# Four seven-product pairs instead of three in every second group of the first feed-forward matrix, weight sums made in place, and an earlier turn of the results

## The chip, the cores and the metric

The kernel runs on one core of one Trainium2 chip. The metric is the device time of one execution in microseconds, from its first instruction to its last. Three runs of the kernel before took 2599.51, 2600.13 and 2600.87 us; their median is 2600.13 us.

## The reference

A trunk of two decoder layers on one sequence of 256 tokens, model width 2048, in float32. Each layer runs a token mixer and then a SwiGLU feed-forward; before each of the two stands an RMS norm with a scale and a shift that are made from a conditioning vector, and the result times a gate is added to the residual. What the change touches is the feed-forward of the second layer (called layer 1):

```python
def swiglu(h, w_in, w_out):
    a, b = jnp.split(h @ w_in, 2, axis=-1)
    return (jax.nn.silu(a) * b) @ w_out
...
        h = (rms_norm(x, norm2_g[i]) * (1.0 + sc2) + sh2).astype(x.dtype)
        x = (x + g2 * swiglu(h, ffn_w_in[i], ffn_w_out[i])).astype(x.dtype)
```

Here `h` is 256 x 2048, `w_in` is 2048 x 11264 (a gate half and an up half of 5632 columns) and `w_out` is 5632 x 2048.

## The kernel before, in words

**Numbers.** Every weight and every activation is held as two rounded parts, `hi` (a cast) and `lo` (the rest), and a product is three matmuls: hi by hi, hi by lo and lo by hi (lines 1188, 1189 and 1190 here, called a triple).

**Feed-forward of layer 1.** Its columns are cut into two parts of 20 and 24 tiles of 128. In each part the first matrix is worked through in groups of four tiles (512 gate columns and 512 up columns with all 2048 rows of `w_in`), then the second matrix with what came out. Group 0 is done in another, narrower form together with the norm (function `normed`); groups 1 to 4 (first part) and 5 to 10 (second part) go through `token_products`: tokens are on the output partitions, 512 weight columns move through TensorE in one matmul. The 2048 rows are taken as eight pairs of 128 rows, 0 to 7. A **plain pair** is 2 rows x 2 column blocks x 2 token halves, each a triple: 24 matmuls of 128x512. A **seven** is the same 2x2x2 block product by Winograd's scheme with seven products in place of eight: 21 matmuls, at the price of sums of weight blocks and of sums of activation blocks. In each of the ten groups three pairs are sevens: 2, 4 and 6. The order of the pairs is 0 to 7, so sevens and plain pairs alternate: P P S P S P S P. The second matrix has twelve sevens more, in three runs of four, never next to one another. A sum over sevens is kept in PSUM banks of its own (m1, m5, m6, m7) and is folded in at the group's end by VectorE (lines 1239 to 1242), after the last seven.

**Weights.** A chunk of 1 MB (128 x 2048: a pair's four blocks of 512, b11, b12, b22, b21 by the order of `Group.blocks`) is loaded by SyncE into one of three `raw` buffers. The function `prepare` makes one piece ready: ScalarE casts `hi` (line 413) and VectorE subtracts to get `lo` (line 416). There are four buffers each of `hi` and `lo` (PART_BUFS). `take`, called by the matmuls, keeps AHEAD = 2 pieces prepared beyond the one in use. A plain pair is two pieces of 1024 columns. A seven is four pieces: p0 with 512 (b11), p1 with 1024, p2 and p3 with 1024 each (sums of blocks). The sums of blocks are made by VectorE in a tile of their own, `sums`: a subtraction of 128x1024 (line 419) after p0, one of 128x512 each at lines 423 and 425; line 425 takes what line 423 made.

**Sums of activations.** `seven_sums` (lines 630 to 642) makes four sums of 128x128 (lines 636 to 639), casts them on ScalarE and subtracts 128x512 (line 642). For the first matrix this is done once for each flagged pair, while the norm's group 0 runs (`modulated`, called by `more` in `normed`); the results are `rows4`, `rows8`, `rows12`. For the second matrix it is done for each pair of tiles that comes out (`msums`, in `turned`).

**A group's end.** What is left after a group's matmuls is queued as asides, which the next group's `token_products` calls by a count (`ticked`): one row of a plain pair, 12 matmuls, counts 8, one product of a seven counts 2. `product_of(0)` is called at a count of 8, `product_of(1)` 8 later and `turned` another 16 later, so at 32, behind the first two plain pairs. `product_of` adds the plain banks to the values (line 1249), takes the silu on ScalarE and multiplies (line 1274); `turned` transposes the result on TensorE (eight matmuls, line 1260) into two banks, from which ScalarE and VectorE make hi and lo (lines 1281, 1282) and, for some tiles, ScalarE copies the bank to `full` (line 1285) for `seven_sums`. These banks are then used for the m sums of the group that runs.

**The end of group 0.** In `normed` the matmuls write two banks, whose reading on VectorE (line 705) comes after `more` has made all rows of `h` (lines 604 and 612, one each for each tile of `h`) and their sums. TensorE's next work (a transpose at line 466 and then the next narrow product) takes such a bank.

The program is written in an order that a tile framework keeps for each engine, with a priority for some instructions. [...]

## Time and profile before

| | us |
|---|---|
| runs shown | 2599.51, 2600.13, 2600.87 |
| median | 2600.13 |
| the profiled execution, whole | 2598.36 |
| its span (first to last instruction) | 2596.6 |
| busy in the span: PE, weight loads | 2566.0, 2237.0 |
| busy in the span: VectorE (DVE), ScalarE (ACT) | 2181.2, 1299.3 |

The profiled execution is 1.77 us under the median, and 1.76 us of it lie outside its span. Its records give start and duration of each instruction; a matmul's records overlap, because the next starts before the last one's end, so that what TensorE needs for one is the distance from start to start. In brackets behind a record stands how long the engine was idle before it, and what released it. The feed-forward of layer 1 lies from about 1871 us to 2583 us of the span; one group of the first matrix takes 42.72 us there.

### The profile page before, as it was taken

The numbers are of one execution on the slowest core, as the hardware profiler recorded it, in microseconds if no ns is written. First come the engines' busy times: TensorE is split into PE (matmuls) and PEld (weight loads), VectorE is DVE, ScalarE is ACT, GpSimd is POOL, SyncE is SP. The second block draws the span as 40 slices with busy tenths as digits, with TensorE's granted clock in tenths as the row PEclk, the third lists the DMA queues.
The fourth block names the chain that finished last, engine by engine and source line by source line (L and its number), as shares of the span: only waits on it lengthen the run. The fifth ranks groups of instructions, "written<-read, shape, count | busy, mean of one in ns | idle before, by whom it ended". The sixth has DMA issues, their size and how long they took to land.

```text
span 2596.6 us, 36680 instructions
## 1 busy us (share of the span) xinstructions
PE 2566.0 (99%) x14329; PEld 2237.0 (86%) x14329; DVE 2181.2 (84%) x2754; ACT 1299.3 (50%) x1757; POOL 133.3 (5%) x230
## 2 busy tenths in 40 slices
PE   7999999999999999999999999999999999999998
PEld 5998889888889888888888898888898888888887
DVE  7998878787698887777878889988899998999984
ACT  5544543444456454334444454444565554555553
POOL 0000000110000011010000000000000000000000
PEclk9999999999999999999999999999999999999999
DMA  9976668777676887878877868877755555555553
GB/s 398 402 279 242 233 240 311 277 294 278 243 296 245 319 339 290 310 286 293 304 296 282 305 242 317 322 289 285 284 185 202 191 207 201 187 203 195 195 197 128
DMA packets 96945, 687.48 MB, mean 265 GB/s; under 512 B 10753, under 2 KB 12545, under 8 KB 13825
## 3 DMA queue, kind: packets, MB, share of 16 engines
q1 hardware_dynamic: 96194, 684.48, 71.2%
q8 instruction: 112, 1.84, 0.3%
q10 hardware_dynamic: 576, 0.66, 0.1%
q14 instruction: 63, 0.52, 0.1%
HBM read 682.99 MB, written 2.10 MB: 264 GB/s over the span
## 4 chain that ended last, share of the span: by engine, by line
PE 70%; issue 28%; DMA 1%; DVE 1%; ACT 0%; SPq 0%; POOL 0%; POOLq 0%; ACTq 0%; DVEq 0%
PE bank L475 30%; PE bank L478 15%; PE bank L513 4%; PE bank L514 4%; PE bank L515 4%; PE bank L498 2%; PE bank L500 2%; PE bank L499 2%; PE bank L543 1%; PE bank L542 1%; PE bank L541 1%; PE bank L688 1%; PE bank L689 1%; PE bank L690 1%; PE bank L1055 1%
## 5 line engine op out<-in xcount | busy, mean ns | idle before, releaser
L413 ACT CAST hi<-raw 128x1024 fp32r<-128x1024 f32 (+1 forms) x912 | 932.5, 1031 | 904.8 <-PE bank L475 312.7
L416 DVE TENSOR_TENSOR lo<-raw,hi 128x1024 fp32r<-128x1024 f32 (+1 forms) x912 | 1081.8, 1196 | 285.6 <-ACT hi L413 283.2
L475 PE MATMUL bank<-h,hi 128*128 128x512 f32 x2016 | 699.8, 391 | 0.0
L478 PE MATMUL bank<-h,lo 128*128 128x256 f32 x2016 | 564.4, 280 | 0.0
L475 PEld LDWEIGHTS bank<-h,hi 128*128 128x128 f32 x2016 | 377.0, 187 | 82.5
L327 DVE SCALAR_TENSOR_TENSOR raw<-raw,cb 128x2048 f32<-128x2048 f32 x160 | 365.8, 2286 | 20.3 <-DMA raw<-w_mod 19.9
L478 PEld LDWEIGHTS bank<-h,lo 128*128 128x128 f32 x2016 | 381.0, 189 | 0.0
L475 PE MATMUL bank<-mid,hi 128*128 128x512 f32 x922 | 320.0, 394 | 0.0
L478 PE MATMUL bank<-mid,lo 128*128 128x256 f32 x922 | 255.4, 277 | 0.0
L475 PEld LDWEIGHTS bank<-mid,hi 128*128 128x128 f32 x922 | 172.9, 188 | 40.1
L513 PE MATMUL bank<-hi,h 128*128 128x512 f32 x512 | 201.5, 394 | 0.0
L514 PE MATMUL bank<-lo,h 128*128 128x512 f32 x512 | 200.6, 392 | 0.0
L515 PE MATMUL bank<-hi,h 128*128 128x512 f32 x512 | 199.7, 390 | 0.0
L1188 PE MATMUL bank<-hi,h 128*128 128x512 f32 x490 | 191.5, 391 | 0.0
L1190 PE MATMUL bank<-hi,h 128*128 128x512 f32 x490 | 190.7, 389 | 0.0
L1189 PE MATMUL bank<-lo,h 128*128 128x512 f32 x490 | 190.7, 389 | 0.0
L475 PE MATMUL bank<-rm,hi 128*128 128x512 f32 x496 | 173.1, 395 | 0.0
L478 PEld LDWEIGHTS bank<-mid,lo 128*128 128x128 f32 x922 | 173.0, 188 | 0.0
L413 ACT CAST hi<-sums 128x1024 fp32r<-128x1024 f32 x84 | 88.4, 1052 | 143.2 <-PE bank L1190 105.4
L416 DVE TENSOR_TENSOR lo<-sums,hi 128x1024 fp32r<-128x1024 f32 x84 | 102.8, 1223 | 50.3 <-ACT hi L413 50.0
L478 PE MATMUL bank<-rm,lo 128*128 128x256 f32 x496 | 137.7, 278 | 0.0
L515 PEld LDWEIGHTS bank<-hi,h 128*128 128x128 f32 x512 | 96.5, 188 | 20.7
(230 smaller groups left out, 4097.8 us busy)
## 6 DMA issues: line engine op xcount, KB each, us to landing
raw<-w_all SPq DMA_DIRECT2D x456, 1024.0 KB, 4.9
raw<-w_mod SPq DMA_DIRECT2D x192, 1024.0 KB, 5.3
x<-x_in SPq DMA_DIRECT2D x4, 512.0 KB, 5.4
decay<-tab_in SPq DMA_DIRECT2D x8, 128.0 KB, 3.3
out<-x SPq DMA_DIRECT2D x4, 256.0 KB, 3.2
out<-x ACTq DMA_DIRECT2D x3, 128.0 KB, 2.6
out<-x SPq DMA_DIRECT2D x1, 384.0 KB, 2.7
out<-x ACTq DMA_DIRECT2D x1, 256.0 KB, 3.2
```

What stands on the lines that cost most here:

```text
L327: nc.vector.scalar_tensor_tensor(raw, raw, 1.0, cb, op0=ALU.mult, op1=ALU.mult, accum_out=total)
L413: nc.scalar.copy(hi[:, :n], raw)
L416: nc.vector.tensor_tensor(lo[:, :n], raw, hi[:, :n].bitcast(F32), op=ALU.subtract)
L475: nc.tensor.matmul(pt, hi, h, start=fresh and k == g.ks[0], stop=False, skip_group_check=True)
L478: nc.tensor.matmul(pt[:, 1, :], lo, h[:, 0, :], start=False, stop=last and k == g.ks[-1], skip_group_check=True)
L498: nc.tensor.matmul(pt, hi, h[:, 0, :], start=first, stop=False, skip_group_check=True)
L513: nc.tensor.matmul(flat(pt), a[:, 0, :], hi, start=first, stop=False)
L514: nc.tensor.matmul(flat(pt), a[:, 0, :], lo, start=False, stop=False)
L515: nc.tensor.matmul(flat(pt), a[:, 1, :], hi, start=False, stop=last)
L1188: nc.tensor.matmul(flat(pt), a[:, 0, :], hi, start=first, stop=False, skip_group_check=True)
L1189: nc.tensor.matmul(flat(pt), a[:, 0, :], lo, start=False, stop=False, skip_group_check=True)
L1190: nc.tensor.matmul(flat(pt), a[:, 1, :], hi, start=False, stop=last, skip_group_check=True)
```

## The change

Pair 5 becomes a seven in every group with an odd number (1, 3, 5, 7 and 9); these groups take the pairs in the order 0, 1, 2, 5, 3, 4, 6, 7, so P P S S P S S P. The groups with an even number keep the three sevens and their order. The sums of weight blocks are written into the raw chunk itself, by four additions of 128x512, and p0 has now 1024 columns (b11, b21) and p1 512 (b22). For that the signs of the activation sums and of the fold at the group's end change, and the order of the seven products. The activation sums are made for four pairs (`rows10` is new). `product_of(0)` is called at once at the group's end, not queued; so `turned` comes at a count of 24 and not 32, which is 12 matmuls earlier. The count of instructions on TensorE goes from 14246 to 14231, on VectorE from 2528 to 2605 and on ScalarE from 1743 to 1756, as the program is built (wait and branch instructions left out); those of GpSimd and SyncE stand as before.

```diff
-IN_SEVENS = {0: (), 1: (2, 4, 6)}
+IN_SEVENS = {0: (), 1: ((2, 4, 6), (2, 5, 4, 6))}
+IN_ORDERS = ((0, 1, 2, 3, 4, 5, 6, 7), (0, 1, 2, 5, 3, 4, 6, 7))
...
-            return [(a, c, DV), (a, d, DV), (b, d, DV), (b, c, DV)]
+            return [(a, c, DV), (b, c, DV), (b, d, DV), (a, d, DV)]
...
-                groups.append(token_group([j * DV, DFF + j * DV], rows, [rows[i] for i in IN_SEVENS[layer]]))
+                order, flagged = IN_ORDERS[j % 2], IN_SEVENS[layer][j % 2]
+                groups.append(token_group([j * DV, DFF + j * DV], [rows[i] for i in order], [rows[i] for i in flagged]))
...
+        b11, b21, b22, b12 = [full[:, n * DV : (n + 1) * DV] for n in range(4)]
...
-            if i < 2:
-                raw = full[:, 2 * DV * i : 2 * DV * i + (DV, 2 * DV)[i]]
-            else:
-                raw = blocks[0][:, 2 * i - 4 : 2 * i - 2, :].rearrange("p a b -> p (a b)")
+            raw = (full[:, :HALF], b22, full[:, HALF:], full[:, :HALF])[i]
...
         if kind == "seven" and i == 0:
-            nc.vector.tensor_tensor(
-                blocks[0][:, 0:2, :].rearrange("p a b -> p (a b)"), full[:, DV : 3 * DV], full[:, : 2 * DV],
-                op=ALU.subtract,
-            )
-            nc.vector.tensor_tensor(t2, block[2], t1, op=ALU.subtract)
+            nc.vector.tensor_tensor(b11, b11, b12, op=ALU.add)
+            nc.vector.tensor_tensor(b12, b12, b22, op=ALU.add)
         elif kind == "seven" and i == 1:
-            nc.vector.tensor_tensor(t4, block[3], t2, op=ALU.subtract)
+            nc.vector.tensor_tensor(b22, b22, b11, op=ALU.add)
+            nc.vector.tensor_tensor(b21, b21, b22, op=ALU.add)
...
-        nc.vector.tensor_tensor(s1, a21, a22, op=ALU.add)
+        nc.vector.tensor_tensor(s1, a21, a22, op=ALU.subtract)
...
-        nc.vector.tensor_tensor(s4, a12, s2, op=ALU.subtract)
+        nc.vector.tensor_tensor(s4, a12, s2, op=ALU.add)
...
-                ("m1", a11), (x_banks[1][0], s4), (x_banks[0][0], a12), ("m5", s1), ("m7", s3), ("m6", s2),
+                ("m1", a11), (x_banks[0][0], a12), (x_banks[1][0], s4), ("m6", s2), ("m7", s3), ("m5", s1),
...
-        return [(8, lambda: product_of(0)), (8, lambda: product_of(1)), (16, turned)]
+        product_of(0)
+        return [(8, lambda: product_of(1)), (16, turned)]
...
-    seven_rows.update(of=(1, 1), pairs=IN_SEVENS[1])
+    seven_rows.update(of=(1, 1), pairs=set(sum(IN_SEVENS[1], ())))
```

Lines 413 and 416 of before are 409 and 412 after; 419, 423 and 425 give way to 415, 416, 418 and 419 (one for each addition); 1188 to 1190 are 1182 to 1184, 1260 is 1254, 1282 is 1276, 1285 is 1279, 705 is 699, and 636 to 639 with 642 are 630 to 633 with 636.

VectorE in group 8 of before, from the end of one seven over a plain pair to the next seven (a `raw` with a number is one chunk, so one pair):

```order
L416 TENSOR_TENSOR lo_22097<-sums_22053,hi_22096 128x1024
L416 TENSOR_TENSOR lo_22109<-raw_22106,hi_22108 128x1024
L419 TENSOR_TENSOR sums_22130<-raw_22128 128x1024
L416 TENSOR_TENSOR lo_22119<-raw_22106,hi_22118 128x1024
L416 TENSOR_TENSOR lo_22132<-raw_22128,hi_22131 128x512
L423 TENSOR_TENSOR sums_22130<-raw_22128,sums_22130 128x512
L416 TENSOR_TENSOR lo_22150<-raw_22128,hi_22149 128x1024
L425 TENSOR_TENSOR sums_22130<-raw_22128,sums_22130 128x512
L642 TENSOR_TENSOR msums_4084_22003<-ssum_21998,msums_4084_22003 128x512
L416 TENSOR_TENSOR lo_22167<-sums_22130,hi_22166 128x1024
L416 TENSOR_TENSOR lo_22174<-sums_22130,hi_22173 128x1024
```

And after, in group 7, from the last two pieces of one seven (chunk raw_21784) to the next (raw_21839):

```order
L412 TENSOR_TENSOR lo_21823<-raw_21784,hi_21822 128x1024
L412 TENSOR_TENSOR lo_21833<-raw_21784,hi_21832 128x1024
L412 TENSOR_TENSOR lo_21842<-raw_21839,hi_21841 128x1024
L412 TENSOR_TENSOR lo_21854<-raw_21839,hi_21853 128x512
L415 TENSOR_TENSOR raw_21839<-raw_21839 128x512
L416 TENSOR_TENSOR raw_21839<-raw_21839 128x512
L418 TENSOR_TENSOR raw_21839<-raw_21839 128x512
L419 TENSOR_TENSOR raw_21839<-raw_21839 128x512
L412 TENSOR_TENSOR lo_21866<-raw_21839,hi_21865 128x1024
L412 TENSOR_TENSOR lo_21876<-raw_21839,hi_21875 128x1024
```

Between two sevens there was a plain pair; now the second seven's pieces follow at once, and its four additions stand together between p1 and p2, where of before's three the first stood ahead of p0 and the last behind p1.

VectorE at the end of group 0 in before (`low` is the read of the norm's product bank, `ssum` and `rows` the activation sums of pair 6):

```order
L637 TENSOR_TENSOR ssum_18445<-ssum_18445,full_18416 128x128
L604 SCALAR_TENSOR_TENSOR u_18471<-x,a_79,rb_18117 128x256
L639 TENSOR_TENSOR ssum_18445<-full_18416,ssum_18445 128x128
L604 SCALAR_TENSOR_TENSOR u_18475<-x,a_79,rb_18117 128x256
L705 TENSOR_TENSOR low_18482<-bank_18016,rb_18117 128x256
L612 SCALAR_TENSOR_TENSOR h<-u_18471,s_83,h 128x256
L642 TENSOR_TENSOR rows_3337_18450<-ssum_18445,rows_3337_18450 128x512
```

And after, at the same place:

```order
L636 TENSOR_TENSOR rows_3330_18396<-ssum_18391,rows_3330_18396 128x512
L606 SCALAR_TENSOR_TENSOR h<-u_18423,s_83,h 128x256
L598 SCALAR_TENSOR_TENSOR u_18451<-x,a_79,rb_18117 128x256
L632 TENSOR_TENSOR ssum_18456<-full_18427 128x128
L598 SCALAR_TENSOR_TENSOR u_18482<-x,a_79,rb_18117 128x256
L598 SCALAR_TENSOR_TENSOR u_18486<-x,a_79,rb_18117 128x256
L606 SCALAR_TENSOR_TENSOR h<-u_18451,s_83,h 128x256
L630 TENSOR_TENSOR ssum_18456<-full_18427 128x128
L606 SCALAR_TENSOR_TENSOR h<-u_18482,s_83,h 128x256
L631 TENSOR_TENSOR ssum_18456<-ssum_18456,full_18427 128x128
L699 TENSOR_TENSOR low_18493<-bank_18016,rb_18117 128x256
```

The new `rows10` (here `rows_3330`) with its four sums stands ahead of that read now, one of pair 6's sums (line 633) has come to stand behind it and one step of `h` (h<-u_18482) ahead of it. Counted over all rows ahead of the read, there are three sums of 128x128, one subtraction of 128x512 and one step of `h` more than before.

TensorE in before, at the place in a group where the results of the group before it are turned (`y` to the transposes, `bank` the PSUM banks; the rows ahead are the end of the second plain pair, the rows behind the first seven's first product):

```order
L1188 MATMUL bank_21207<-hi_21230,h 128x512
L1189 MATMUL bank_21207<-lo_21231,h 128x512
L1190 MATMUL bank_21207<-hi_21230,h 128x512
L1260 MATMUL bank_21288<-tab,y_3913_21162 128x128
L1260 MATMUL bank_21288<-tab,y_3915_21164 128x128
...
L1188 MATMUL bank_21316<-hi_21253,h 128x512
L1189 MATMUL bank_21316<-lo_21254,h 128x512
L1190 MATMUL bank_21316<-hi_21253,h 128x512
```

And after: the transposes stand 12 matmuls ahead of the end of the second plain pair.

```order
L1182 MATMUL bank_21597<-hi_21600,h 128x512
L1183 MATMUL bank_21597<-lo_21601,h 128x512
L1184 MATMUL bank_21597<-hi_21600,h 128x512
L1254 MATMUL bank_21656<-tab,y_3974_21548 128x128
L1254 MATMUL bank_21656<-tab,y_3976_21550 128x128
...
L1182 MATMUL bank_21594<-hi_21620,h 128x512
L1183 MATMUL bank_21594<-lo_21621,h 128x512
L1184 MATMUL bank_21594<-hi_21620,h 128x512
```

Of the eight transposes two are shown in each.

More of the change, by code (lines that the diff above doesn't have):

```diff
@@ L401, in prepare @@
         else:
-            if i == 0:
-                blocks[:] = [spool[0].tile([P, 4, DV], F32, tag="sums", name=name("sums"), bufs=1)]
-            block = [full[:, n * DV : (n + 1) * DV] for n in range(4)]
-            t1, t3, t2, t4 = [blocks[0][:, n, :] for n in range(4)]
-            if i < 2:
-                raw = full[:, 2 * DV * i : 2 * DV * i + (DV, 2 * DV)[i]]
-            else:
-                raw = blocks[0][:, 2 * i - 4 : 2 * i - 2, :].rearrange("p a b -> p (a b)")
+            raw = (full[:, :HALF], b22, full[:, HALF:], full[:, :HALF])[i]
         hi = wpool.tile([P, HALF], F32R, tag="hi", name=name("hi"))
@@ L418, in prepare @@
         if kind == "seven" and i == 0:
-            nc.vector.tensor_tensor(
-                blocks[0][:, 0:2, :].rearrange("p a b -> p (a b)"), full[:, DV : 3 * DV], full[:, : 2 * DV],
-                op=ALU.subtract,
-            )
-            nc.vector.tensor_tensor(t2, block[2], t1, op=ALU.subtract)
+            nc.vector.tensor_tensor(b11, b11, b12, op=ALU.add)
+            nc.vector.tensor_tensor(b12, b12, b22, op=ALU.add)
         elif kind == "seven" and i == 1:
-            nc.vector.tensor_tensor(t4, block[3], t2, op=ALU.subtract)
-    blocks, spool = [], []
+            nc.vector.tensor_tensor(b22, b22, b11, op=ALU.add)
+            nc.vector.tensor_tensor(b21, b21, b22, op=ALU.add)
+    spool = []
     prepared = [0]
@@ L1240, in token_products @@
                 nc.vector.tensor_tensor(y21, m7, y12, op=ALU.add)
-                nc.vector.tensor_tensor(y12, m5, y12, op=ALU.add)
-                nc.vector.tensor_tensor(y22, m5, y21, op=ALU.add)
+                nc.vector.tensor_tensor(y12, m5, y12, op=ALU.subtract)
+                nc.vector.tensor_tensor(y22, m5, y21, op=ALU.subtract)
         x11, x12, x21, x22 = [flat(x_banks[c][t]) for t in range(2) for c in range(2)]
```

## The prediction

> **What bounds the kernel now.** I read the page first, for the share of each engine.
>
> ```profile
> span 2596.6 us, 36680 instructions
> PE 2566.0 (99%) x14329; PEld 2237.0 (86%) x14329; DVE 2181.2 (84%) x2754; ACT 1299.3 (50%) x1757; POOL 133.3 (5%) x230
> PEclk9999999999999999999999999999999999999999
> ```
>
> TensorE (PE) is busy 99% of the span, at full granted clock in every slice. The kernel lasts as long as TensorE's matmuls and the few gaps between them, so a matmul that is taken out is worth its whole distance, and any new wait of TensorE costs its whole length. VectorE (DVE) stands at 84% over the span, but the change works in one stage, so I cut two stretches out: one group of the first matrix, and the end of the norm's group 0.
>
> ```profile
> core 0: us, PE busy (x) PEld busy (x) DVE busy (x) ACT busy (x) POOL busy (x), PEclk, DMA share, GB/s
> 2248.00:2291.00 43.00, 42.95 (x194) 35.33 (x193) 39.79 (x49) 24.82 (x29) 0.00 (x0) 1.00 0.57 196
> 1884.00:1907.00 23.00, 23.00 (x193) 23.00 (x192) 23.00 (x52) 18.54 (x33) 0.00 (x0) 1.00 0.47 166
> ```
>
> In a group with three sevens VectorE is already busy 39.79 of 43.00 us: 3.2 us are left. At the end of group 0 nothing is left, 23.00 of 23.00. VectorE is thus the engine that could take the bound over. The waits, from 1926 to 2463 us, tell who waits for whom in the groups today:
>
> ```profile
> engine line waited for: us in total, times, longest us
> ACT hi L413 <- PE bank L1190: 190.6, 142, 2.6
> DVE lo L416 <- ACT hi L413: 46.7, 43, 1.6
> PEld bank L1188 <- ACT full L1285: 3.8, 8, 0.5
> ```
>
> The weight pieces wait for TensorE: a cast cannot begin until a `hi` buffer, one of four, has been read for the last time. Weight loads wait for ScalarE only eight times. No row shows TensorE waiting for `lo`. So the lookahead is set by the buffers, not by spare time.
>
> **The change part by part: matmuls taken out.** The distance of two matmuls, and one of the eight bank waits, in group 8:
>
> ```profile
> 2337.27 0.39 PE L1188 MATMUL bank<-hi,rows 128*128 128x512 f32 x1
> 2337.50 0.39 PE L1189 MATMUL bank<-lo,rows 128*128 128x512 f32 x1
> 2337.73 0.39 PE L1190 MATMUL bank<-hi,rows 128*128 128x512 f32 x1
> 2338.17 0.50 PE L1188 MATMUL bank<-hi,rows 128*128 128x512 f32 x1
> ```
>
> Start to start is 0.23 (0.46 for two; over longer stretches 0.2267). Five plain pairs of 24 become sevens of 21: 15 matmuls less, 15 x 0.2267 = **-3.40 us**, all on the path.
>
> **The earlier turn.** Between 2337.73 and 2338.17 lie 0.44 us in place of 0.23: 0.21 are lost because a bank is still being copied by ScalarE (the row L1188 <- L1285 above). The transposes now stand 12 matmuls, 12 x 0.2267 = 2.72 us, earlier, far more than 0.21, so all eight waits go: 8 x 0.21 = **-1.7 us**. What the transposes need is made by `product_of(1)`, which has moved up by the same count (from 16 to 8, the turn from 32 to 24), so I cost no new wait there.
>
> **The entry.** VectorE and TensorE at the end of group 0:
>
> ```profile
> 1905.22 0.29 DVE L638 TENSOR_TENSOR ssum<-full 128x128 f32<-128x128 f32 x1
> 1905.42 0.28 DVE L637 TENSOR_TENSOR ssum<-ssum,full 128x128 f32<-128x128 f32 x1
> ...
> 1906.62 0.42 DVE L705 TENSOR_TENSOR low<-bank,rb 128x256 f32<-128x256 f32 x1
> 1906.95 0.47 DVE L612 SCALAR_TENSOR_TENSOR h<-u,s,h 128x256 fp32r<-128x256 f32 x1
> 1907.35 0.69 DVE L642 TENSOR_TENSOR rows<-ssum,rows 128x512 fp32r<-128x512 f32 x1
> 1907.95 0.42 DVE L705 TENSOR_TENSOR low<-bank,rb 128x256 f32<-128x256 f32 x1
> ```
>
> ```profile
> 1907.12 0.29 PE L690 MATMUL bank<-h,lo 128*128 128x258 f32 x1
> 1907.25 0.27 PE L466 MATMUL bank<-tab 128*128 128x128 f32 x1
> ```
>
> The first read of a norm bank runs from 1906.62 to 1907.04, and TensorE's next work in that bank starts at 1907.25, right behind its last matmul (1907.12): 0.2 us of margin. VectorE was full in the 23 us before, so what comes ahead of that read moves it by its whole length: three sums at 0.20 (1905.22 to 1905.42), one 128x512 at 0.60 (1907.35 to 1907.95), one step of `h` at 0.40: 1.60 us. The read then starts at 1908.22, ends at 1908.64, and TensorE goes on 0.05 later, at 1908.69 and not 1907.25: **+1.44 us**. The other sum of pair 6 and its subtraction queue behind the read and are wanted only in group 1. Bounds: nothing, if some of those 23 us are stretched by waits between VectorE's own operations that the new ones fill; 1.6, if there is no margin at all.
>
> **Two sevens in a row.** This is the large term. Rows of VectorE in a group of before, and of the buffer chain:
>
> ```profile
> 2328.04 0.68 DVE L416 TENSOR_TENSOR lo<-raw,hi 128x512 fp32r<-128x512 f32 x1
> 2328.64 0.68 DVE L1274 TENSOR_TENSOR y<-y,y 128x512 f32<-128x512 f32 x1
> 2329.24 1.22 DVE L419 TENSOR_TENSOR sums<-raw 128x1024 f32<-128x1024 f32 x1
> 2330.38 1.22 DVE L416 TENSOR_TENSOR lo<-raw,hi 128x1024 fp32r<-128x1024 f32 x1
> 2331.51 0.69 DVE L423 TENSOR_TENSOR sums<-raw,sums 128x512 f32<-128x512 f32 x1
> 2332.23 0.69 DVE L425 TENSOR_TENSOR sums<-raw,sums 128x512 f32<-128x512 f32 x1
> 2332.95 1.23 DVE L416 TENSOR_TENSOR lo<-sums,hi 128x1024 fp32r<-128x1024 f32 x1
> 2335.67 1.22 DVE L416 TENSOR_TENSOR lo<-sums,hi 128x1024 fp32r<-128x1024 f32 x1 [1.49 <-ACT hi L413]
> ```
>
> ```profile
> 2334.11 0.39 PE L1190 MATMUL bank<-hi,h 128*128 128x512 f32 x1
> ...
> 2334.59 1.05 ACT L413 CAST hi<-sums 128x1024 fp32r<-128x1024 f32 x1 [1.67 <-PE bank L1190]
> ```
>
> A 128x1024 takes 1.13 on VectorE (2330.38 to 2331.51), a 128x512 0.60 (2328.04 to 2328.64), and one that takes the result of the operation before it 0.72 (2331.51 to 2332.23). The cast of a free buffer starts 0.08 after TensorE's last matmul with it (2334.50 to 2334.59), takes 1.05, and `lo` follows 0.04 later.
>
> Now the second of two adjacent sevens. Its p0 takes the buffers of the first one's p0, four pieces back. Let that p0's last matmul end at 0; the next began at -0.16, and 15 matmuls of the first seven are left. ScalarE casts p0 from 0.08 to 1.13. VectorE: `lo` of p0 from 1.17 to 2.30, `lo` of p1 (128x512) to 2.90, then the four additions in a chain, each waiting for the one before: 2.90, 3.62, 4.34 (ends 5.03), 5.06. p2 is made of the blocks that the third addition completes, so its cast runs from 5.07 to 6.12, its `lo` from 6.16 to 7.38, and TensorE can use it from 7.42. Without a stall TensorE wants it 15 + 6 (p0) + 3 (p1) + 1 = 25 matmuls after -0.16, which is 25 x 0.2267 - 0.16 = 5.51. The stall is 7.42 - 5.51 = **1.91 us**. Queued behind these additions are only the later pieces, which follow TensorE at their usual distance.
>
> Behind a plain pair the same chain has 15 matmuls more: a plain pair is two pieces, so p0 takes the buffer of the seven before, p2, and 6 + 24 + 6 + 3 + 1 = 40 matmuls lie between. 40 x 0.2267 - 0.16 = 8.91, which is 1.5 us later than 7.42. That is the work which hides the chain where sevens alternate, and why the three-seven groups pay nothing although their sums became a longer chain too.
>
> There are two adjacent pairs in each of five groups, ten in all. In groups 3, 7 and 9 a `msums` subtraction of 128x512 stands between the first and the second addition of the first pair: 0.60 in place of the 0.12 of dependence, +0.48. Sum: 7 x 1.91 + 3 x 2.39 = **+20.5 us**. A second road gives the same size: VectorE's work for a four-seven group is 4 plain pairs x 2 x 1.13 = 9.0, 4 sevens x (3 x 1.13 + 0.60 + 4 x 0.72) = 27.5, and the group's end, 12 operations of 512 (four each at lines 1239 to 1242 and 1249, two each at 1274 and 1282) x 0.60 = 7.2: 43.7 us, against 180 x 0.2267 = 40.8 plus eight transposes (0.8) on TensorE. VectorE no longer fits, by 2.1 us, before any wait for a cast.
>
> The Trainium skill ("VectorE: DVE Perf Modes", section "The DRAIN you can't avoid") says that the flush of the pipeline follows every VectorE operation anyway, and that a semaphore between chained operations costs nothing on top. By that rule the additions would stand 0.60 apart, the third would end 0.24 sooner and the ten stalls would come to some 18.1 us in all. The rows above show 0.72 for a dependent 128x512 and 0.60 for an independent one, and I go by them.
>
> The bounds of one pair: if the chain packs as tightly as independent work does and no cast is waited for, `lo` of p2 starts at 2.90 + 4 x 0.60 = 5.30 and TensorE waits 5.30 + 1.26 - 5.51 = 1.05. Upward, TensorE also has to load weights behind a wait: the bank wait above shows 0.2 of that, 2.1. A gain is excluded: no piece becomes ready sooner than its buffer is free.
>
> **Sum.** -3.40 - 1.7 + 1.44 + 20.5 = +16.8. Profiled execution 2598.36 + 16.8 = 2615.2. The median of the runs shown, 2600.13, is 1.77 above the profiled one, so in its frame **2617.0 us**.
>
> **Rivals.** *Not slower: the additions are hidden.* If the second seven's pieces are made ahead of time, there is no stall: 2598.36 - 3.40 - 1.7 + 1.44 + 1.77 = 2596.5, no change that can be told. It decides at one place, p2 of the second seven: `lo` must be ready 5.5 us after the first seven's p0 is free, not 7.4. For it: VectorE keeps 3.2 us idle in a group today and TensorE never waits for `lo`. Against it: the casts wait 142 times for TensorE's L1190, so nothing can be made ahead of a free buffer, and the 1.9 us missing are more than the handoffs in the chain (0.04 each) can give. Chance 0.11.
>
> *Slower still: VectorE sets the pace in the other five groups too.* There the first seven's third addition (L418) now stands behind the `mids` subtractions that wait for the transposes, and by the same ledger its p2 has some 0.3 us of margin where `msums` come in between. Should that be lost, each of these groups pays up to what an adjacent pair does, 5 x 1.9 = 9.5: 2626.5. For it: VectorE's 39.79 of 43.00 grows by 0.1 to 0.2 a seven. Against it: the transposes come 2.72 us earlier. Chance 0.10.
>
> **How the numbers follow.** The forecast has 0.76, the two rivals 0.11 and 0.10, and 0.03 stay for a gain that I see no way to. A measurement of this kernel tells about 0.2% from no change, 5.2 us. All gains together without entry or stall are -5.1, so faster by over 0.2% has that 0.03; within 0.2% is the first rival, 0.11; slower is the forecast and the second rival, 0.86. Range: the low end takes 1.05 for a pair (7 x 1.05 + 3 x 1.65 = 12.3) and nothing for the entry: 2598.36 - 5.1 + 12.3 + 1.77 = 2607.3, less the 0.6 to 0.7 by which the shown runs stray from their median, rounded to 2606. The high end takes in the second rival: 2627. It leaves out the first rival.
>
> **What would show it.** Right: in the groups 1, 3, 5, 7 and 9 TensorE waits twice for `hi` and `lo` (lines 409 and 412) at the first product of p2 of the seven behind a seven, some 1.9 us each time, ten times, and nowhere else in the groups; the rows L1188 <- L1285 are gone from the waits; a group with four sevens lasts about 45 us, one with three 42.3; the first L699 starts near 1908.2. Wrong: no wait of TensorE for line 412 (first rival), or such waits in the groups with even numbers (second), or more matmul time at a granted clock below 1.00.

## The result, and the profile after

The changed kernel takes 2623.33 us (median of 4 runs, 2620.24 to 2624.46) against 2599.82 us before (4 runs): a ratio of 1.0086 with a 95% interval of 1.0074 to 1.0099. It is slower by 0.9%. The forecast was 2617.0, with 2606 to 2627.

The page of the profiled execution after (2620.24 us whole), its span, engines and granted clock:

```profile
span 2618.5 us, 36768 instructions
PE 2568.2 (98%) x14314; PEld 2235.2 (85%) x14314; DVE 2215.8 (85%) x2831; ACT 1306.6 (50%) x1770; POOL 128.2 (5%) x230
PEclk9999999999999999999999999999999999999999
```

TensorE has 15 instructions less, and the span is 21.9 us longer. Nothing on this page tells where; a group with four sevens (group 7) and one with three (group 6) do, as two windows (the columns are the length, then busy time and instructions of each engine, the granted clock, the transfers' share and rate):

```profile
core 0: us, PE busy (x) PEld busy (x) DVE busy (x) ACT busy (x) POOL busy (x), PEclk, DMA share, GB/s
2303.70:2348.90 45.20, 41.59 (x182) 33.41 (x181) 43.29 (x56) 26.16 (x31) 0.00 (x0) 1.00 0.47 171
2261.30:2303.70 42.40, 42.40 (x193) 35.20 (x192) 40.64 (x53) 25.11 (x29) 0.00 (x0) 1.00 0.55 203
```

With three sevens TensorE has no gap. With four it is idle for 3.6 of 45.2 us, while VectorE is busy for all but 1.9. The waits of TensorE in the feed-forward of layer 1, from 1926 to 2490 us:

```profile
PEld bank L1182 <- ACT hi L409: 14.3, 11, 1.7
PEld bank L1183 <- DVE lo L412: 10.7, 10, 1.1
```

The row for the bank that ScalarE copies is gone. Ten times TensorE waits for the cast and ten times for the subtraction of a weight piece; the eleventh time of the first row is a weight load's 0.2 us in the second matrix, at 2167.77, which delays no matmul. One of the ten places is p2 of the second adjacent seven in group 1's second pair of sevens. VectorE, ScalarE and TensorE there:

```profile
1955.22 0.69 DVE L415 TENSOR_TENSOR raw<-raw 128x512 f32<-128x512 f32 x1
1955.94 0.69 DVE L416 TENSOR_TENSOR raw<-raw 128x512 f32<-128x512 f32 x1
1956.66 0.69 DVE L418 TENSOR_TENSOR raw<-raw 128x512 f32<-128x512 f32 x1
1957.39 0.69 DVE L419 TENSOR_TENSOR raw<-raw 128x512 f32<-128x512 f32 x1
1958.52 3.50 DVE L412 TENSOR_TENSOR lo<-raw,hi 128x1024 fp32r<-128x1024 f32 x3 [0.44 <-ACT hi L409]
```

```profile
1957.44 3.90 ACT L409 CAST hi<-raw 128x1024 fp32r<-128x1024 f32 x4 [0.43 <-DVE raw L418]
```

```profile
1957.36 0.39 PE L1184 MATMUL bank<-hi,rows 128*128 128x512 f32 x1
1958.54 0.50 PE L1182 MATMUL bank<-hi,rows 128*128 128x512 f32 x1 [0.80 <-ACT hi L409]
1959.80 0.50 PE L1183 MATMUL bank<-lo,rows 128*128 128x512 f32 x1 [0.76 <-DVE lo L412]
1960.14 0.40 PE L1184 MATMUL bank<-hi,rows 128*128 128x512 f32 x1
```

The additions stand 0.72 apart (1955.22, 1955.94, 1956.66, 1957.39). The cast of p2 starts 0.09 after the third has ended (1957.35 to 1957.44), the subtraction at 1958.52. TensorE would have begun at 1957.36 + 0.23 = 1957.59. It waits 0.96 for the cast, 1.03 for the subtraction, and 0.11 more until its spacing is regular again: 2.10 us, as for all waits below unless the 0.11 is said to be left out.

The end of group 0, VectorE and TensorE:

```profile
1910.76 0.28 DVE L631 TENSOR_TENSOR ssum<-ssum,full 128x128 f32<-128x128 f32 x1
1910.96 0.41 DVE L699 TENSOR_TENSOR low<-bank,rb 128x256 f32<-128x256 f32 x1
```

```profile
1909.86 0.28 PE L684 MATMUL bank<-h,lo 128*128 128x258 f32 x1
1911.52 0.30 PE L460 MATMUL bank<-tab 128*128 128x128 f32 x1 [1.38 <-DVE low L699]
```

From 1909.86 to 1911.52 there are 1.66 us where 0.12 is the usual distance: 1.54 lost to the read of the norm's bank. The matmul at 1909.86 is the one that started at 1907.12 before, so 2.74 us of the longer span were lost ahead of this place; the account below comes back to them.

### The profile page after: what moved, and what is told of

Read it like the earlier page. It is cut to its first block, busy times and chain, and to the rows that moved or that the text cites. A ratio compares the mean times of both kernels' runs of the same rounds, so it can differ in the third digit from the quotient of the medians.

```text
span 2618.5 us, 36768 instructions
## 1 busy us (share of the span) xinstructions
PE 2568.2 (98%) x14314; PEld 2235.2 (85%) x14314; DVE 2215.8 (85%) x2831; ACT 1306.6 (50%) x1770; POOL 128.2 (5%) x230
## 3 DMA queue, kind: packets, MB, share of 16 engines
q8 instruction: 112, 1.84, 0.3%
## 4 chain that ended last, share of the span: by engine, by line
PE 66%; issue 29%; DMA 3%; DVE 2%; ACT 0%; SPq 0%; POOL 0%; POOLq 0%; ACTq 0%; DVEq 0%
PE bank L469 28%; PE bank L472 14%; PE bank L507 4%; PE bank L508 4%; PE bank L509 4%; DMA raw<-w_all 2%; PE bank L494 1%; PE bank L492 1%; PE bank L493 1%; PE bank L537 1%; PE bank L536 1%; PE bank L535 1%; PE bank L682 1%; PE bank L683 1%; PE bank L684 1%
## 5 line engine op out<-in xcount | busy, mean ns | idle before, releaser
L409 ACT CAST hi<-raw 128x1024 fp32r<-128x1024 f32 x1006 | 1021.0, 1031 | 1007.2 <-PE bank L469 308.4
L412 DVE TENSOR_TENSOR lo<-raw,hi 128x1024 fp32r<-128x1024 f32 x1006 | 1186.0, 1196 | 311.2 <-ACT hi L409 305.5
L507 PE MATMUL bank<-hi,h 128*128 128x512 f32 x512 | 201.4, 393 | 0.0
L508 PE MATMUL bank<-lo,h 128*128 128x512 f32 x512 | 200.8, 392 | 0.0
L509 PE MATMUL bank<-hi,h 128*128 128x512 f32 x512 | 199.9, 390 | 0.0
L1182 PE MATMUL bank<-hi,h 128*128 128x512 f32 x465 | 181.7, 391 | 0.0
L1184 PE MATMUL bank<-hi,h 128*128 128x512 f32 x465 | 181.0, 389 | 0.0
L1183 PE MATMUL bank<-lo,h 128*128 128x512 f32 x465 | 181.0, 389 | 0.0
L509 PEld LDWEIGHTS bank<-hi,h 128*128 128x128 f32 x512 | 96.6, 189 | 20.7
L507 PEld LDWEIGHTS bank<-hi,h 128*128 128x128 f32 x512 | 96.8, 189 | 17.7
L469 PEld LDWEIGHTS bank<-rm,hi 128*128 128x128 f32 x496 | 93.0, 188 | 21.8
```

Of the source, the lines that this page charges most:

```text
L409: nc.scalar.copy(hi[:, :n], raw)
L412: nc.vector.tensor_tensor(lo[:, :n], raw, hi[:, :n].bitcast(F32), op=ALU.subtract)
L469: nc.tensor.matmul(pt, hi, h, start=fresh and k == g.ks[0], stop=False, skip_group_check=True)
L507: nc.tensor.matmul(flat(pt), a[:, 0, :], hi, start=first, stop=False)
L508: nc.tensor.matmul(flat(pt), a[:, 0, :], lo, start=False, stop=False)
L509: nc.tensor.matmul(flat(pt), a[:, 1, :], hi, start=False, stop=last)
```

## The experiments

In each the edit is against the changed kernel, unless another one is named. Each time stands beside runs of the kernel before on the same chip (2600.8, 2600.66 and 2600.92 us for the three sets, in the order below).

**Three sevens everywhere, the rest of the change kept.**

```diff
-IN_SEVENS = {0: (), 1: ((2, 4, 6), (2, 5, 4, 6))}
-IN_ORDERS = ((0, 1, 2, 3, 4, 5, 6, 7), (0, 1, 2, 5, 3, 4, 6, 7))
+IN_SEVENS = {0: (), 1: ((2, 4, 6), (2, 4, 6))}
+IN_ORDERS = ((0, 1, 2, 3, 4, 5, 6, 7), (0, 1, 2, 3, 4, 5, 6, 7))
```

> Three sevens (pairs 2, 4, 6) in every group, in the order 0 to 7; the sums in place, the signs and the earlier turn stay. Theory (a seven right behind a seven is what costs, because the cast and the subtraction of its pieces can start only when a buffer comes free): no wait of TensorE for line 412 is left, the eight bank waits of 0.32 stay away, the entry pays nothing since there is no fourth set of activation sums: 2599.8 - 2.5 = 2597.3 us. Rival (the in-place additions cost by themselves, in every seven, because they stand in one chain): waits of TensorE for line 412 remain in some sevens behind plain pairs, and the time stays above 2600.

Measured: 2597.67 us (11 runs), a ratio to before of 0.9990, 0.9981 to 0.9999. From 1874 us to 2583 us no matmul starts more than 0.1 us later than its usual distance. The additions in place and the longer chain cost nothing where a plain pair stands between; the earlier turn is worth what the eight waits were: from the end of group 0 to the end of the last group the trace is 2.8 us shorter than before, and the eight waits were 2.5. It is the fastest version of the study, faster than the kernel before by 0.1%, with an interval that just leaves out no change.

**Three sevens, two of them adjacent in five groups.**

```diff
-IN_SEVENS = {0: (), 1: ((2, 4, 6), (2, 5, 4, 6))}
-IN_ORDERS = ((0, 1, 2, 3, 4, 5, 6, 7), (0, 1, 2, 5, 3, 4, 6, 7))
+IN_SEVENS = {0: (), 1: ((2, 4, 6), (2, 4, 6))}
+IN_ORDERS = ((0, 1, 2, 3, 4, 5, 6, 7), (0, 1, 2, 4, 3, 6, 5, 7))
```

> Three sevens in every group, so as much work for VectorE as in the kernel before, but in groups 1, 3, 5, 7 and 9 two of them stand next to one another (order 0, 1, 2, 4, 3, 6, 5, 7 with 2, 4, 6 as sevens: P P S S P S P P). Theory (adjacency with four buffers): five waits of 2.1 to 2.6 us at p2 of the second seven, 12.3 us in all, 2597.3 + 12.3 = 2609.6 us. Rival (it is the sum of VectorE's work in a group with four sevens, 43.7 us against 41.6, that costs, wherever the sevens stand): no wait, 2597.3 us.

Measured: 2616.26 us (5 runs), ratio 1.0057 (1.0044 to 1.0069). The five waits are where they were expected, 2.0, 2.5, 2.4, 2.5 and 2.5 us without the 0.11 behind each, and the number of sevens, and so VectorE's work, is that of the run above: adjacency costs, not the count. (Four sevens apart from one another can't be tried: `token_products` takes none at the first or the last place, and of the six places between, at most three lie apart.) But the time is 6.7 us above the 2609.6 expected. Group 3's place on TensorE shows why:

```profile
2026.45 0.39 PE L1184 MATMUL bank<-hi,rows 128*128 128x512 f32 x1
2028.14 0.50 PE L1182 MATMUL bank<-hi,rows 128*128 128x512 f32 x1 [1.30 <-ACT hi L409]
2029.40 0.72 PE L1183 MATMUL bank<-lo,rows 128*128 128x512 f32 x1 [0.76 <-DVE lo L412]
2029.92 0.63 PE L1184 MATMUL bank<-hi,rows 128*128 128x512 f32 x1
2030.34 0.63 PE L1182 MATMUL bank<-hi,rows 128*128 128x512 f32 x1
...
2032.48 0.60 PE L1184 MATMUL bank<-hi,rows 128*128 128x512 f32 x1
2032.90 0.41 PE L1182 MATMUL bank<-hi,h 128*128 128x512 f32 x1
2033.15 0.40 PE L1183 MATMUL bank<-lo,h 128*128 128x512 f32 x1
```

Behind the wait matmuls follow one another in 0.42 to 0.43 us (2029.92 to 2030.34), not 0.23, until 2032.9, although no wait is shown. Windows of 3.41 us around three of the five waits give the granted clock; in the windows' columns it stands third from the end:

```profile
2026.13:2029.54 3.41, 1.35 (x6) 0.58 (x5) 2.88 (x5) 2.50 (x3) 0.00 (x0) 0.99 0.12 48
2029.54:2032.95 3.41, 3.41 (x9) 2.63 (x10) 3.22 (x4) 2.43 (x3) 0.00 (x0) 0.50 0.40 108
2220.66:2224.08 3.42, 2.25 (x10) 1.50 (x8) 2.86 (x6) 1.09 (x2) 0.00 (x0) 1.00 0.30 125
2224.08:2227.49 3.41, 2.65 (x10) 1.99 (x11) 3.41 (x4) 3.41 (x4) 0.00 (x0) 1.00 0.12 14
1937.37:1940.79 3.42, 1.84 (x8) 0.99 (x7) 2.92 (x4) 2.74 (x3) 0.00 (x0) 1.00 0.18 77
1940.79:1944.20 3.41, 3.41 (x10) 2.63 (x9) 3.41 (x4) 2.19 (x3) 0.00 (x0) 0.50 0.35 132
```

After a window in which TensorE was busy 1.35 or 1.84 of 3.41 us the clock is 0.50 for one window; that costs about 8 matmuls x 0.2 = 1.6 us. After windows with 2.25 and 2.65 busy (the wait in group 5, of 2.4 us, lies across a boundary) it stays at 1.00. Four of the five waits are followed by such a stretch; added up over the matmuls of the trace they cost 6.1 us, nearly all of the 6.7 that was missing.

**One addition of four.**

```diff
         if kind == "seven" and i == 0:
-            nc.vector.tensor_tensor(b11, b11, b12, op=ALU.add)
-            nc.vector.tensor_tensor(b12, b12, b22, op=ALU.add)
+            pass
         elif kind == "seven" and i == 1:
             nc.vector.tensor_tensor(b22, b22, b11, op=ALU.add)
-            nc.vector.tensor_tensor(b21, b21, b22, op=ALU.add)
```

> As the changed kernel, but three of the four additions of weight blocks are left out in every seven (only b21's neighbour, the addition to b22, stays), so that the sums of blocks are not made and the output is another one. It shortens the chain between p1 and p2 by two additions of 0.72, and takes 2.2 us of VectorE's work out of each seven. Theory (the chain behind a freed buffer): the ten waits shrink by 1.44 and do not vanish, from 2.1 to some 0.8 each, 8 to 9 us in all: 2623.3 - 14 = 2609 us. Rival (VectorE's work in the group): with 43.7 - 8.6 = 35 us VectorE fits easily into 41.6, all waits go: 2600.4 us.

Measured: 2606.1 us (10 runs), ratio 1.0022 (1.0013 to 1.0032). All ten waits are left, six of 0.7 and four of 1.0 us without the 0.11, and none is followed by a slow stretch. The theory's shape holds (2609 expected): in the trace the ten waits fall from 22.9 to 9.3 us, 13.5 less. The medians differ by 17.2; the mean granted clock, 0.997 or 0.998 in all ten runs where three of the changed kernel's four have 0.996, fits that the slow stretches of the changed kernel, below, are gone as well. The rival's 2600.4 is excluded.

**No activation sums for pair 5.**

```diff
-                        g, lambda k: h[k], lambda k: seven_rows[k],
+                        g, lambda k: h[k], lambda k: seven_rows[8 if k == 10 else k],
...
-    seven_rows.update(of=(1, 1), pairs=set(sum(IN_SEVENS[1], ())))
+    seven_rows.update(of=(1, 1), pairs={2, 4, 6})
```

> As the changed kernel, but the activation sums of pair 5 are not made; those of pair 4 stand in for them, so the output is another one. Theory: the read of the norm's bank (line 699) has no more ahead of it than in the kernel before, the wait of 1.54 us at the end of group 0 goes: 2623.3 - 1.5 = 2621.8 us, and the ten waits stay. Rival (the wait there has another cause, such as the other order of the sums): 2623.3 us.

Measured: 2619.02 us (4 runs), ratio 1.0071 (1.0057 to 1.0085). The wait at the end of group 0 is gone from the trace, the ten others are there, with one stretch at half clock. The 4.3 us on the medians are more than the 1.54 of the trace. The mean granted clock is 0.997 in three of the four runs here and 0.996 in three of the changed kernel's four, so slow stretches may make up part of it; the spread of both kernels' runs (2.6 and 4.2 us) doesn't allow more to be read from them.

**Five buffers each of hi and lo**, on top of the edit above.

```diff
-PART_BUFS = 4
+PART_BUFS = 5
```

> As the run without pair 5's activation sums (those of pair 4 stand in, so the output is another one; this frees the space), with five buffers each of hi and lo in place of four. Theory (the chain starts when a buffer comes free): p0 of the second seven can start 6 matmuls, 1.36 us, sooner; the first wait of each group shrinks to about 1, the second, which comes on top of VectorE's load, to about 2; some 7 us less in all than with four buffers: 2619.0 - 7 = 2612 us, and fewer stretches at half the granted clock. Rival (VectorE's work in a group is the bound): one more buffer changes next to nothing, 2619 us.

Measured: 2611.65 us (4 runs), 7.4 less than with four buffers; ratio 1.0043 (1.0028 to 1.0058). The first wait of each group falls from 2.0 to 2.5 us to 0.7 to 1.1, the second, 2.0 before, is 1.8 to 2.6 (without the 0.11), and one stretch at half clock is left. So the buffers set when the chain starts, and VectorE's load takes part behind the first pair: in group 3, between the two waits (2025.4 to 2041.1 us), VectorE has one gap of 0.47 us and none other above 0.04. Both theories hold a piece here.

**The turn at 32.**

```diff
-        product_of(0)
-        return [(8, lambda: product_of(1)), (16, turned)]
+        return [(8, lambda: product_of(0)), (8, lambda: product_of(1)), (16, turned)]
```

> As the changed kernel, with the asides as before: product_of(0) after a count of 8, the turn at 32. Theory: the eight bank waits of 0.32 us return, 2623.3 + 2.5 = 2625.8 us, and the ten waits stay as they are. Rival (the turn has nothing to do with the bank waits, or they hide in the new ones): 2623.3 us.

Measured: 2625.07 us (4 runs), ratio 1.0094 (1.0079 to 1.0109). Against the changed kernel's 1.0086 the difference lies inside the intervals; the trace holds eight waits at the turn's banks, four of 0.47 and four of 0.19 us, each with 0.11 behind it (3.5 us in all), and two stretches at half clock; the ten waits come to 22.1 us, 0.7 less than with the earlier turn. That the bank waits come back is seen, their worth isn't measured by the medians; the run with three sevens bounds it better.

**Two additions on GpSimd.** p2 becomes b11 + b12 and b12 + b22 in a tile of their own, p3 the blocks b21 and b22 in place, and the products follow that order.

```diff
-            raw = (full[:, :HALF], b22, full[:, HALF:], full[:, :HALF])[i]
+            if i == 0:
+                blocks[:] = [spool[0].tile([P, 2, DV], F32, tag="sums", name=name("sums"), bufs=1)]
+                nc.gpsimd.tensor_tensor(blocks[0][:, 0, :], b11, b12, op=ALU.add)
+                nc.gpsimd.tensor_tensor(blocks[0][:, 1, :], b12, b22, op=ALU.add)
+            two = blocks[0].rearrange("p a b -> p (a b)")
+            raw = (full[:, :HALF], b22, two, full[:, DV : 3 * DV])[i]
...
-            nc.vector.tensor_tensor(b11, b11, b12, op=ALU.add)
-            nc.vector.tensor_tensor(b12, b12, b22, op=ALU.add)
...
-            nc.vector.tensor_tensor(b22, b22, b11, op=ALU.add)
+            nc.vector.tensor_tensor(b22, b22, blocks[0][:, 0, :], op=ALU.add)
...
-                ("m1", a11), (x_banks[0][0], a12), (x_banks[1][0], s4), ("m6", s2), ("m7", s3), ("m5", s1),
-                (x_banks[0][1], a22),
+                ("m1", a11), (x_banks[0][0], a12), (x_banks[1][0], s4), ("m5", s1), ("m7", s3),
+                (x_banks[0][1], a22), ("m6", s2),
```

> Four sevens in the order of the changed kernel, with two of the four additions of weight blocks on GpSimd, which is idle in this stage: b11 + b12 and b12 + b22 go into a tile of their own as soon as the chunk has landed, and make p2; VectorE makes only b22 and b21 in place after p1, and they make p3. The products stand in an order that fits. Theory (the chain between the freed buffer and p2 sets the wait): p2 needs none of VectorE's additions any more, its lo is ready at about 5.5 us after the first seven's p0 is free, which is when TensorE wants it, and VectorE's work in the group falls from 43.7 to 38 us: at most some 0.3 us of each wait is left, 2599.8 - 3.4 - 2.5 + 1.5 = 2595.4, up to 2599. Rival (four sevens in a group don't fit, or GpSimd's additions are too slow or slow VectorE down): waits of 1 us and more remain, 2608 or above.

Measured: 2639.35 us (4 runs), ratio 1.0149 (1.0132 to 1.0166). The expectation failed, and the rival it named came true. GpSimd's two additions of 128x512 in the whole program (busy, mean):

```profile
L408 POOL TENSOR_TENSOR sums<-raw 128x512 f32<-128x512 f32 x47 | 90.2, 1919 | 0.0
L407 POOL TENSOR_TENSOR sums<-raw 128x512 f32<-128x512 f32 x47 | 65.4, 1391 | 494.9 <-DMA raw<-w_all 314.4 <-DVE lo L417 126.9 <-ACT hi L414 40.7
```

And two kinds of 128x512 on VectorE in the first four groups (shortest, median and longest in ns); the first takes one input from a bank, the second both from SBUF, and the third line is this second one in the changed kernel:

```profile
L1245 DVE TENSOR_TENSOR y<-bank,y x16: 673/678/681, 1967.6 to 2109.8; 128x512 f32<-128x512 f32 x16
L1270 DVE TENSOR_TENSOR y<-y,y x7: 677/1770/1780, 1970.5 to 2107.5; 128x512 f32<-128x512 f32 x7
L1268 DVE TENSOR_TENSOR y<-y,y x8: 681/683/693, 1970.1 to 2103.9; 128x512 f32<-128x512 f32 x8
```

The one with an input in PSUM keeps its 0.68 us, the one with both in SBUF takes 1.77 where GpSimd is at work: from 1926 to 2480 us, the nine of this kind that lie beside an addition of GpSimd take 1.77 to 1.79, the nine others 0.67 to 0.68. VectorE's subtractions of 128x1024, which have both inputs in SBUF too, take up to 2.3 there and 1.2 elsewhere. How much of the time lost comes from GpSimd's own length and how much from VectorE's isn't separated.

**The activation sums on GpSimd too**, on top of that (the four `nc.vector.tensor_tensor` of `seven_sums` become `nc.gpsimd.tensor_tensor`).

> As the run with two additions on GpSimd, and the four sums of 128x128 of seven_sums on GpSimd too, for the first matrix and the second. Theory: the read of the norm's bank at the end of group 0 has 15 operations of 0.2 us less of VectorE ahead of it, so the wait of 1.54 us there goes: 2595.4 - 1.5 = 2593.9 us. Rival (GpSimd is slow on such small operations, and the last pair's sums come too late): a wait of some us at the entry or at the first seven, 2597 or above.

Measured: 2672.39 us (4 runs), ratio 1.0275 (1.0259 to 1.0290). A miss of the same kind: the wait at the end of group 0 grows to 5.0 us, and behind the waits 64 matmuls stand 0.43 us from the next.

**Matmuls of zeros in the place of the wait**, on top of the run with three sevens, two of them adjacent. The product before p2 gets FILL matmuls more, whose weights are zeros.

```diff
+FILL = 9
...
+    zero_row = fpool.tile([P, P], F32R, tag="zero", name="zero")
+    nc.scalar.activation(zero_row, ones, AF.Identity, scale=0.0)
...
             for i, (to, a) in enumerate(plan):
+                if i == 3 and steps[n - 1].seven:
+                    for _ in range(FILL):
+                        nc.tensor.matmul(
+                            flat(x_banks[1][0]), zero_row, parts[0], start=False, stop=False, skip_group_check=True
+                        )
                 parts = take(g, i, None, DV)
```

> As the run with three sevens of which two are adjacent in five groups, and in front of p2 of each second seven nine matmuls of 128x512 with zeros as weights into a bank that is being summed (they add nothing): 9 x 0.227 = 2.04 us of work in the place of the wait. Theory (TensorE's clock is halved for some 3.5 us after a wait that leaves it idle for most of 2 to 2.5 us): the pieces come no sooner, so the waits of 2.1 to 2.6 us are filled and at most 0.5 us of each remains, and no matmul stands 0.43 apart any more: 2616.3 less 4 x 1.7 to 1.9 = 2609 us. Rival (the slow matmuls behind a wait have another cause, such as transfers or banks that come late): they stay, 2616 us.

> The same with four such matmuls, 0.91 us of work, and 1.2 to 1.7 us of waiting left. Theory: the sum of work and waiting is the same, and TensorE is idle for at most 1.7 us at a time: no stretch at half clock or at most one, 2609 to 2611 us. Rival: 2616 us.

Measured: 2610.85 us with nine and 2610.45 us with four (4 runs each; ratios 1.0043, 1.0029 to 1.0057, and 1.0041, 1.0027 to 1.0055), where the same kernel without them takes 2616.26 (1.0057, 1.0044 to 1.0069). No matmul stands 0.43 apart in these groups any more. The same two windows of group 3 as above, with nine:

```profile
2026.10:2029.54 3.44, 3.14 (x14) 2.28 (x13) 2.97 (x4) 3.44 (x5) 0.00 (x0) 1.00 0.00 0
2029.54:2032.95 3.41, 3.41 (x16) 2.81 (x15) 3.41 (x4) 1.66 (x3) 0.00 (x0) 1.00 0.76 264
```

Nothing is ready sooner, and more work is done. From the end of group 0 to the end of the last group the trace with nine is 6.2 us shorter than the one without, and the four slow stretches there were 6.1: what is gained is the clock's.

**The changed kernel with nine matmuls of zeros at its ten places, and the changed kernel again.** (The edit is the one above, on the changed kernel; the second has none.)

> The changed kernel with the nine matmuls of zeros in front of p2 of each second seven, ten places. Theory: the runs of the changed kernel that lie above the profiled one (2620.2; median 2623.3) had one or two stretches at half clock of 1.4 to 1.9 us each; with the waits filled there are none, and the median falls to about 2620 to 2621 us although nothing is done sooner. Rival (the runs differ for another reason, such as the transfers around 1810 us): 2623.3 us.

> The changed kernel itself once more, beside the run with the matmuls of zeros. Theory: 2623 us, above that run by 2 to 3 us, and if its profile holds stretches at half clock, its time less 1.4 to 1.9 for each is that of the first profile, 2620. Rival: 2623 us, the same as the filled one.

Measured, side by side: 2619.62 us filled (5 runs, 2617.77 to 2620.96; ratio 1.0073, 1.0060 to 1.0086) and 2622.12 us unfilled (5 runs, 2618.85 to 2623.73; ratio 1.0084, 1.0070 to 1.0097). The difference, 2.5 us, is what the theory says, but the intervals overlap. The unfilled one's profiled run had one slow stretch and was yet its fastest, 2618.85. From the end of group 0 to the end of the last group the filled trace is 17.1 us longer than before, the first profile of the changed kernel 17.1 and its second one 18.8, which is 17.3 without the 1.6 of its stretch. So the three agree where no stretch lies. The mean granted clock is 0.997 or 0.998 in all five filled runs and 0.996 in the four unfilled ones that weren't profiled.

## Why the prediction was right, and where its sizes were off

The mechanism was right: ten waits at p2 of the second adjacent seven, none elsewhere in the groups, the cast and then the subtraction, at the place the ledger gave. By its steps:

| step | forecast, us | trace after, us |
|---|---|---|
| 15 matmuls less | -3.40 | -3.40 |
| eight bank waits gone | -1.7 | -2.5 |
| the read at the end of group 0 | +1.44 | +1.54 |
| ten waits behind adjacent sevens | +20.5 | +22.9 |
| sum | +16.8 | +18.5 |

- **The ten waits** are the term that was mis-sized, by 2.4 us. Each plain one is 2.10, not 1.91. On the ledger's clock (0 at 1952.30) the additions start within 0.03 us of it, but the cast of p2 starts 0.09 and not 0.04 behind the third addition, and TensorE's first matmul with `lo` at 7.50 and not 7.42: 0.08. The other 0.11 is behind the wait: the matmul there lasts 0.50 us and not 0.39 (its weight load of 0.19 starts only with it), and the next comes 0.34 later and not 0.23. The prediction's upper bound, 2.1, had this 0.2, but read it off a bank wait, which was the wait itself. Group 5's first pair, forecast as plain, took 2.5: four operations of line 1295, which read what the second matrix left, stand ahead of `lo` of p0 and put it off by 1.35 us, of which eight transposes on TensorE give 0.95 back. Groups 3, 7 and 9 took 2.6 where 2.39 was forecast, the same 0.2. With the turn at 32 the `msums` come later and the first pairs of these groups take 2.0, the second 2.4: the surcharge moved with them, as the step said.
- **The read at the end of group 0** moved by the 1.60 us that were forecast (to 1910.96; less the 2.74 lost ahead of it, 1908.22). TensorE went on 0.15 behind its end and not 0.05.
- **The bank waits** cost 0.31 each and not 0.21. Behind each of them a second gap of 0.10 follows (2338.17 to 2338.50 before); I had priced only the first. (Two more weight loads had waited 0.2 us each, for a cast; "only eight times" left them out.)
- **The dependent additions** stood 0.72 apart, as the rows of before had it. By the rule of the Trainium skill ("VectorE: DVE Perf Modes", section "The DRAIN you can't avoid") it would have been 0.60; the trace decides for the rows. (The sum by that rule is 18.5 and not 18.1: where the `msums` stand between the additions, only 0.12 and not 0.24 would fall away.)
- **The first rival** (hidden additions) fell: TensorE waits at each of the ten places. **The second** (the other five groups pay too) fell as well: in the even groups no matmul starts late (group 6 in the windows above), and the run with three sevens none in any group.
- **The second road** did not give the same size, as the prediction said: 2.1 us a group in five groups is 10.5, not 20.5. VectorE was busy 43.29 us in group 7, near the 43.7 worked out, but the group took 45.20; the load is not the whole cost.
- **What the prediction had left out** is the rest. The measured medians differ by 23.5 us, the profiled executions by 21.9, and the trace's terms give 18.5. One part is in the profile, the 2.74 us that are lost before the end of group 0; some 0.6 more is spread over the span. Most of the 2.74 lies at one place: at 1810 us, ahead of the change's code, TensorE waits for a weight piece that came late (its chunk's transfer was issued at 1801.22, where before issued it at 1797.61).

```profile
1810.40 0.39 PE L469 MATMUL bank<-mid,hi 128*128 128x512 f32 x1
1812.40 0.39 PE L472 MATMUL bank<-mid,lo 128*128 128x256 f32 x1 [1.61 <-DVE lo L412]
```

Here 1.77 us are lost, and 0.11 behind it; another 0.7 is lost in the 25 us ahead of it, in small steps. In the other traces of this study the same place loses from nothing (the kernel before, the changed one's second profile) to 1.87 us (three sevens), with the same code up to there, so I count it as an accident and not as the change's. The other part is the clock: a wait of 2 to 2.6 us can halve it for the 3.4 us behind, and the changed kernel has ten such waits. In the groups the first profile had no such stretch, its second one, the run without pair 5's sums and the one with five buffers one each, the turn at 32 two. For the runs without a profile the mean granted clock is known: 0.996 in the other three of the first four, where the profiled one has 0.997. One stretch takes 0.5 x 3.41 / 2618 = 0.00065 off the mean, so these three had about two stretches more, some 3 us, and the median of the four is 3.1 above the profiled one. With the waits filled no run has 0.996, and the kernel takes 18.7 us more than the one before on the same chip, close to the 18.5 of the sum. So the remaining 2 to 3 us of the medians fit the clock; where the stretches of the unprofiled runs lay isn't shown.

I had named a granted clock below 1.00 as a sign that would prove me wrong; it came in the experiments and, by the mean clock, in the unprofiled runs, as an addition to the waits and not in their place.

## What to carry to other kernels

Behind a fixed number of buffers, preparation has no lookahead beyond them: what counts is how much work the consumer has between the moment a buffer comes free and the moment the new piece is wanted, here 24 matmuls against 39. Two expensive items in a row cut that cover, even when the mean load of the preparing engine stays the same, so items are to be ordered by cover before they are added. A saving of three matmuls (0.68 us) can't pay for a wait of 2.1, and a wait of 2 us can cost another 1.6 through the clock.

## What the runs showed of the hardware that was not expected

**The clock falls after short idling, on a fixed grid.** In the kernel with adjacent sevens the slow stretches end at 1944.20, 2032.95, 2316.26 and 2404.98 us (worked out from the one matmul in each whose distance to the next lies between 0.23 and 0.43). They lie 26, 83 and 26 times 3.413 us apart, to within 0.03. So the clock is decided here in windows that run on by themselves and don't move with the waits. Whether a wait is followed by a slow stretch depends on how it lies in them: in that kernel, windows with TensorE busy 1.84 of 3.41 us and less were followed by half clock, those with 2.25 and more were not. The changed kernel's first profile shows that the busy time of the records is not the measure; two of its windows with 1.87, and the one behind the second:

```profile
2027.65:2031.06 3.41, 1.87 (x8) 0.97 (x6) 2.88 (x5) 1.84 (x2) 0.00 (x0) 1.00 0.33 137
2420.18:2423.59 3.41, 1.87 (x7) 1.34 (x8) 2.97 (x4) 3.41 (x4) 0.00 (x0) 1.00 0.00 0
2423.59:2427.00 3.41, 3.41 (x17) 2.81 (x16) 3.41 (x4) 2.19 (x3) 0.00 (x0) 1.00 0.72 247
```

The run with two additions on GpSimd even has one with 1.66 (from 1941.47) that is followed by 1.00, and one with 1.77 (from 2327.17) that is followed by 0.50. What does part them is the matmuls counted at their usual distance, 0.2267 us for 512 columns and in proportion for fewer. I laid the grid of 3.413 us through each of the 14 traces, from 100 us to 2583 us, and counted the windows at full clock: all 18 with up to 1.3 us of matmuls were followed by half clock, and none with 1.36 or more. So in these kernels the limit lay at 38 to 40% of a window, about six matmuls of 128x512.

The Trainium skill ("TensorE: Matmul & The Clock Gate", "Part 1: The HAM clock gate") tells of a free-running window of 3413 ns and of half the clock after an idle one; the runs agree with the length and the half, 0.50, but show that a window need not be idle from end to end.

**GpSimd's work slows VectorE's.** An operation of VectorE with both inputs in SBUF went from 0.68 to 1.77 us beside GpSimd's additions, one with an input in PSUM stayed at 0.68. GpSimd took 1.4 to 1.9 us in the mean for a 128x512 that VectorE does in 0.6; its shortest took 1.27, and most of the second additions, which meet VectorE's work, 2.28. The Trainium skill ("GPSIMD Engine Reference", section 1, Specifications) says that GpSimd's way to SBUF is shared with VectorE and that VectorE's instructions with two SBUF inputs meet contention; the trace agrees. My expectation had it only as a rival, without a size.
